# The last norm's factor from a matrix of ones, and two background transfers placed later, in a one-core residual block

## The chip, the core and the metric

The kernel runs on one core of one Trainium2 chip. The engines that appear below are TensorE (PE, with its weight loads PEld), VectorE (DVE), ScalarE (ACT), GpSimd (POOL) and SyncE (SP), which only issues transfers here. Every time is in device microseconds (us) of one execution of the whole program. Before the change the median of three runs is 695.37 us (695.27 to 695.41).

## The reference

One trunk layer on x of 512 tokens by 1024 features, in float32, and a last RMSNorm. What matters here is the second half:

```
h = rms_norm(x, norm_ffn_g)
up = causal_dwconv(h @ w_up, conv_ffn_w)        # 1024 -> 2 * 2816, three taps
a, b = split(up, 2)
x = x + (silu(a) * b) @ w_down                  # 2816 -> 1024
return rms_norm(x, norm_f_g)                    # x / sqrt(mean(x*x) + 1e-6) * g
```

Ahead of it stand a first norm, one wide projection, a short gated convolution, forgetting attention, two sigmoid gates and an output projection w_o.

## The kernel before, in words

**Layout.** Features lie on the 128 partitions, tokens along the free dimension: x is a tile `xm` (also called x1) of 8 blocks of 128 features by 512 tokens. A sum over features is a sum over partitions, so the kernel makes it on TensorE, with a matrix or a column of ones.

**Arithmetic.** Each weight chunk is loaded as float32 (`raw_...`), and split into a high part `wh_...` (ACT, L275) and a rest `wl_...` (DVE, L279). A product is then three matmuls: high by high, rest by high, high by rest. The activations are split in the same way: `gh` and `gl` hold the hidden activations, `x1h` and `x1l` the normed input.

**The stream of weights.** All chunks stand in one list in the order of use. `split()` loads ahead on SP's queue (up to 7 chunks, in buffers of 4 per kind) and makes the two parts of the next chunk. A load waits until its buffer's last chunk has been split. Everything on SP's queue starts in the order in which it stands there.

**Seven products in place of eight.** Many products go through `seven()`, in which a pair of output blocks and input blocks is worked off with seven half-size products on sums of weights and activations. For these a chunk comes in two pieces: `P{n}`, loaded straight from the weights `wst`, and `F{n}` ("full"), which holds sums of weights. Those sums are made in the background in DRAM tiles `f{n}`, two values of n to a tile, by `make_forms()`: a copy into the tile on SP, an adding transfer on POOL, a copy within the tile on SP, an adding transfer on POOL, another copy and another adding transfer. Each of the six waits for the one before it. `slot()` is called at fixed places of the program, counts them, and issues the operations that are due. `GROUPS` gives, for each set of sums, how many n to a tile, the slots of the six operations, and how many slots later the next tile's start.

**The feed-forward part.** The 22 hidden blocks of 128 run in two phases (0 to 11, 12 to 21). Block j is made in `up(j, ...)`, two calls of `slot()` each. A phase ends with steps through `seven()` that multiply by w_down: 12 steps of one P and one F in phase 0 (P18/F18 to P29/F29), with one `slot()` each. The output projection before has 8 slots, so block 11 has slots 30 and 31 and the steps of phase 0 have 32 to 43. Blocks 14 and 16 in phase 1 go through `seven()` too; their sums are the tiles `f30` and `f32` ("phase 1's sums"), which are made during phase 0. The key is `"up1"`.

**Where a phase turns.** Work that takes finished sums out of TensorE's banks waits in a list `later` and is handed out between splits. Entries with the tag `("e",)` belong to blocks that went through `seven()`. At the last block of a phase, `up()` splits the first P chunk; if entries with that tag are still there, it also hands all of them out and splits the first F chunk.

**The end.** The last two output blocks are finished in two halves of 256 tokens. For each half, `ssq3` collects the sums of squares per partition, with the very last block's squares in `sq3_...` apart. `rstd_col()` turns them into a column: matmuls with the squares as weights and one column of ones (L344) put the 256 tokens on partitions, as 128 by 2; ACT takes the root (L350), DVE the reciprocal (L352). `rstd_bc()` (L363) spreads the column back over all partitions with matmuls against the identity into a bank `pb_n31`. `fin_out()` then multiplies the 8 blocks by it in five instructions on DVE (L1412), and sends each piece to DRAM from SP or ACT (L1413). `warm_on(n)` puts n matmuls into TensorE's queue whose results nobody reads.

Of the kernel before, what the change touches and what calls it, by code (L numbers as in the profile page):

```python
# [8 lines left out]
F32 = mybir.dt.float32  # L9
F32R = mybir.dt.float32r  # L10
AF = mybir.ActivationFunctionType
ALU = mybir.AluOpType

P = 128
D = 1024
S = 512
KB = D // P
# [25 lines left out]
PHASES = ((0, 12), (12, NP))  # L43
# [20 lines left out]
DOUBLES = GATES + UPD[0] + STEPS[0] + UPD[1] + STEPS[1]  # L64
NU = [len(GATES), len(GATES + UPD[0] + STEPS[0])]
ND = [NU[i] + len(UPD[i]) for i in range(2)]
GROUPS = {"gate": (2, 4, 1), "up0": (2, 4, 1), "up1": (2, 4, 1), 0: (2, (0, 3, 14, 18, 22, 26), 1), 1: (2, 3, 1)}


@with_exitstack  # L70
def block_kernel(ctx, tc, xT, vecs, wv, win, wmix, wo, wup, wst, wdp, outT):
# [3 lines left out]
    nc = tc.nc  # L75
    PSUM = bass.MemoryType.PSUM

    cp = ctx.enter_context(tc.tile_pool(name="cp", bufs=1))
# [3 lines left out]
    def keep(ins):  # L82
        return tc.keep_in_program_order(ins)

    def bank(i, name):
        return ps.tile([P, S], F32, tag=f"b{i}", name=name)
# [19 lines left out]
    ones = cp.tile([P, P], F32, tag="ones", name="ones")  # L106
# [52 lines left out]
    def after_split():  # L159

        st = ExitStack()
        for ins in order.values():
            st.enter_context(tc.issue_after(ins))
        return st

    def tag_of(k):
        return "raw" if stream[k][0][0] != "F" else "rf" if k >= ff0 else "rg"
# [22 lines left out]
    def make_forms(n0, n1, key, start=0):  # L190

        size, step, shift = GROUPS[key]
        if not start:
            make_forms.slot = 0
        cuts = [n0]
        for n in range(n0 + 1, n1 + 1):
            if n == n1 or n - cuts[-1] == size or len(DOUBLES[n]) != len(DOUBLES[cuts[-1]]):
                cuts.append(n)
        for g, (a, b) in enumerate(zip(cuts, cuts[1:])):
            m = len(DOUBLES[a]) * P  # L200
            f = dr.tile([P, b - a, 4 * m], F32, tag=f"f{a}", name=f"f{a}")
            w = wst[a:b].rearrange("n p c -> p n c")
            x0, x1, x2 = w[:, :, 3 * m : 5 * m], w[:, :, 5 * m : 7 * m], w[:, :, 7 * m : 8 * m]
            for n in range(a, b):
                made[n] = f[:, n - a, :]

            def put(dst, src):
                return lambda: keep(nc.sync.dma_start(dst, src))

            def add(dst, src):  # L210
                return lambda: keep(nc.gpsimd.dma_start(dst, src, accum_op=ALU.add))  # L211

            f0, f1, f2 = f[:, :, : 2 * m], f[:, :, 2 * m : 3 * m], f[:, :, 3 * m :]
            ops = (put(f0, x0), add(f0, x1), put(f1, f[:, :, :m]), add(f1, x1[:, :, m:]), put(f2, f1), add(f2, x2))
            todo_bg.extend((start + (step * k if isinstance(step, int) else step[k]) + shift * g, op) for k, op in enumerate(ops))
        todo_bg.sort(key=lambda w: w[0])
# [7 lines left out]
    def run_later(k, us):  # L224

        n = 0
        while n < len(later):
            if later[n][0] <= k and later[n][1] <= us + 0.1:
                us -= later[n][1]
                with after_split():  # L230
                    later.pop(n)[3]()
            elif later[n][0] <= k:
                return
            else:
                n += 1
# [11 lines left out]
    def flush_only(tags):  # L247

        while n := [n for n, w in enumerate(later) if set(w[2]) & set(tags)]:
            with after_split():  # L250
                later.pop(n[0])[3]()

    def split(hl=None):

        k = len(parts)
        if k == len(stream):
            return
        nm, _, ncol = stream[k]
        load(k + (LOOK if len(raws) > KB else AHEAD))
        if hl is None:  # L260
            hl = []
            for x in "hl":
                if k == 0:
                    wp.tile([P, PADW[x]], F32, tag=f"pad{x}", name=f"pad_{x}")
                w0 = VOFF if k < KB else 0
                hl.append(wp.tile([P, D], F32R, tag=f"w{x}", name=f"w{x}_{nm}", bufs=2)[:, w0 : w0 + ncol])
        hi, lo = hl
        raw = raws[k]
        if k == 0:
            for cs in (slice(VB, S + H), slice(0, VB)):  # L270
                keep(nc.vector.tensor_copy(hi[:, cs], raw[:, cs]))
        elif k == 1:
            keep(nc.vector.tensor_copy(hi, raw))
        else:
            ins = nc.scalar.activation(hi, raw, AF.Copy)  # L275
            order["hi"] = ins.ins
            if k < KB:
                keep(ins)
        ins = nc.vector.tensor_sub(lo, raw, hi.bitcast(F32))  # L279
        order["lo"] = ins.ins  # L280
        if k < KB:
            keep(ins)
        held[tag_of(k)] -= 1
        parts.append((hi, lo))
        if any(("e",) in w[2] for w in later):
            run_later(k, {"u": 4.2, "P": 1.6, "F": 1.2}[nm[0]])
            return
        run_later(k, {"u": 1.7, "P": 1.6, "F": 0.75, "i": 3.0, "m": 3.0, "d": 0 if nm == "dp1" else 2.1}.get(nm[0], 3.5))
# [47 lines left out]
    eps = ex[:, NT : NT + 1]  # L336
# [22 lines left out]
    def rstd_bc(rc, n, bb, name):  # L359

        pb = bank(bb, f"pb_{name}")
        for t in range(n):
            keep(nc.tensor.matmul(  # L363
                pb[:, t * P : (t + 1) * P], rc[:, t : t + 1].to_broadcast([P, P]), ident,
                start=True, stop=True,
            ))
        return pb
# [49 lines left out]
    pb = [pb_[t // 2][:, (t % 2) * 4 * HD : (t % 2 + 1) * 4 * HD] for t in range(NT)]  # L417
# [13 lines left out]
    halves = [slice(0, S // 2), slice(S // 2, S)]  # L431
# [20 lines left out]
    for kb in range(KB):  # L452
        x = xs[kb]
# [320 lines left out]
    for q in (0, 2):  # L774
        f, g = x_sums(slice(q, q + 2))
# [8 lines left out]
    for idx in late:  # L784
        kind, i = divmod(idx, 4)
# [311 lines left out]

    po = None
    make_forms(ND[0], ND[0] + len(STEPS[0]), 0)
    make_forms(NU[1], ND[1], "up1", 20)  # L1100
    for j in range(KB):
        slot()
        if j == 0:
# [32 lines left out]
    ssq3 = xp.tile([P, S], F32, tag="ssq", name="ssq3")  # L1136
# [4 lines left out]
    def up(j, ph, rb2, pu=None):  # L1141
        uu = []

        def tap(i, z):
            u = fp.tile([P, S], F32, tag="fu", name=f"fu{j}{i}", bufs=3)
            taps(u, z, CF + 3 * (2 * j + i))
            uu.append(u)

        if j in SUP[ph]:
            c = 2 * SUP[ph].index(j)  # L1150
            slot()
            seven(
                UPD[ph][c : c + 2], NU[ph] + c, {j: USETS[j]}, lambda q, g: up_form(ph, q, g), of="x",
                done=lambda i, banks, ids: merge(ph, j, banks, ids, rb2, tap, uu),
            )
            slot()
            return
        evacs = []
        for i in range(2):
            slot()  # L1160
            p = pu[i] if pu else block(f"up{2 * j + i}", x1h, x1l, True)
            if i and j + 1 == PHASES[ph][1]:
                split_next()
                if any(("e",) in w[2] for w in later):
                    flush_only((("e",),))
                    split()
            z = [None]

            def mul(i=i, p=p, z=z):
                z[0] = fp.tile([P, S], F32, tag="fz", name=f"fz{j}{i}", bufs=4)  # L1170
                nc.vector.tensor_mul(z[0], p, rb2)

            evac = [(0.7, mul), (1.4, lambda i=i, z=z: tap(i, z[0]))]
            if i:
                evac.append((0, lambda: glu(ph, j, uu)))
            if any(("e",) in w[2] for w in later):
                later.extend((0, us, (("e",), acc.last) if x == 0 else (("e",),), f) for x, (us, f) in enumerate(evac))
            else:
                for _, f in evac:
                    f()  # L1180
# [221 lines left out]
    def fin_col(t, sqs):  # L1402
        s_ = ssq3[:, halves[t]]
        nc.vector.tensor_add(s_, s_, sqs[0])
        return rstd_col([s_, sqs[1]], 2, 3 + t, f"n3{t}", root=True)

    def fin_out(t, rc):
        hs = halves[t]
        pb = rstd_bc(rc, 2, (1, 5)[t], f"n3{t}")[:, : S // 2]
        for g, (a, b) in enumerate(((0, 1), (1, 3), (3, 5), (5, 7), (7, 8))):  # L1410
            y = x1[:, a:b, hs]
            nc.vector.tensor_mul(y, y, pb.unsqueeze(1).to_broadcast([P, b - a, S // 2]))  # L1412
            keep((nc.sync, nc.scalar)[g % 2].dma_start(outT[:, a:b, hs], y))  # L1413
# [10 lines left out]
    plain7(0, 1, kall[:7])  # L1424
    rcA = fin_col(0, sqA)
    plain7(0, 1, kall[7:])
    fin_out(0, rcA)
    sqB = [fin_sum(1, 0)]
    plain7(1, 1, kall[:4])
    for x in range(2):  # L1430
# [1 line left out]
    plain7(1, 1, kall[4:])  # L1432
    sqB.append(fin_sum(1, 1))
    warm_on(3)
    rcB = fin_col(1, sqB)
    warm_on(6)
    fin_out(1, rcB)


_INS = ["xT", "vecs", "wv", "win", "wmix", "wo", "wup", "wst", "wdp"]  # L1440
# [96 lines left out]
```

## Time and profile before

| | |
|---|---|
| median of 3 runs | 695.37 us (695.27 to 695.41) |
| the profiled execution | 694.18 us, of which 692.4 us from the first to the last instruction |
| granted TensorE clock | 0.997 |
| TensorE busy | 683.1 us (99%) |
| VectorE busy | 554.2 us (80%) |
| ScalarE busy | 368.3 us (53%) |
| GpSimd busy | 190.5 us (28%) |

A row of a group view gives the line, the engine, the operation, the tiles as out<-in with their numbers left out, shapes, the count, then busy time and mean ns of one, and the idle time before with what ended it. A row of a timeline gives start, duration, engine, line, tiles and shapes, merged where equal ones follow each other; a matmul in float32 shows as two instructions. Rows with SPq or ACTq are transfers being issued, so their duration is not the transfer's.

### The profile page before, as it was taken

What the parts mean: (1) busy time and instruction counts of PE and PEld (TensorE: products, weight loads), DVE (VectorE), ACT (ScalarE), POOL (GpSimd) and SP (SyncE); (2) the same over time, 40 slices, a digit from 0 to 9 for tenths busy, and PEclk for the clock granted to TensorE, in tenths of its full rate; (3) what the DMA queues carried; (4) which work ended last, traced back from release to release, by engine and by line L of the source; (5) the groups of instructions that cost most, each with busy time, mean ns of one, the idle gap of its engine ahead of it and who ended that gap; (6) DMA issues with size and microseconds to landing.
All of it is one profiled execution on the core that took longest, in us unless ns stands there. A gap on an engine that the chain in (4) does not pass through costs nothing. (4 is left out here: it accounts for less than half of the span.)

```text
span 692.4 us, 14690 instructions
## 1 busy us (share of the span) xinstructions
PE 683.1 (99%) x5936; PEld 680.6 (98%) x5936; DVE 554.2 (80%) x858; ACT 368.3 (53%) x579; POOL 190.5 (28%) x201
## 2 busy tenths in 40 slices
PE   9999999999999999999999999999999999999996
PEld 9999999999999999999999999999999999999995
DVE  6677787877578778769879699998787899988894
ACT  5675755554554444546554555545444544545572
POOL 6134947542020201214400144340100325231000
PEclk9999999999999999999999999999999999999998
DMA  8629999552568586788998498888945996676413
GB/s 308 225 67 293 216 243 204 134 120 92 185 144 221 166 268 205 230 308 213 158 313 241 126 233 222 200 242 231 252 149 167 337 231 157 188 168 182 154 31 122
DMA packets 65012, 137.53 MB, mean 199 GB/s; under 512 B 5760, under 2 KB 30352, under 8 KB 64688
## 3 DMA queue, kind: packets, MB, share of 16 engines
q1 hardware_dynamic: 44664, 107.28, 47.2%
q0 software_dynamic: 18464, 26.03, 23.4%
q10 hardware_dynamic: 1816, 3.29, 1.3%
q8 instruction: 46, 0.75, 0.4%
q14 instruction: 22, 0.18, 0.1%
HBM read 132.31 MB, written 47.71 MB: 260 GB/s over the span
## 5 line engine op out<-in xcount | busy, mean ns | idle before, releaser
L211 POOL DMA_DIRECT2D f<-in_wst_dram x66 | 77.7, 1371 | 27.1 <-DMA f<-f 26.8
L309 PE MATMUL p_up<-x1h,wh_up 128*128 128x256 f32 x416 | 81.2, 276 | 0.0
L309 PE MATMUL p_up<-x1l,wh_up 128*128 128x256 f32 x416 | 81.0, 276 | 0.0
L309 PE MATMUL p_up<-x1h,wl_up 128*128 128x256 f32 x416 | 81.0, 276 | 0.0
L279 DVE TENSOR_TENSOR wl_F<-raw_F,wh_F 128x1024 fp32r<-128x1024 f32 (+1 forms) x42 | 55.9, 1330 | 20.0 <-ACT wh_F L275 20.0
L275 ACT ACTIVATE wh_F<-raw_F 128x1024 fp32r<-128x1024 f32 (+1 forms) x42 | 44.3, 1054 | 39.5 <-PE dn L327 28.7
L309 PEld LDWEIGHTS p_up<-x1h,wh_up 128*128 128x128 f32 x416 | 62.7, 188 | 0.0
L309 PEld LDWEIGHTS p_up<-x1l,wh_up 128*128 128x128 f32 x416 | 62.7, 188 | 0.0
L309 PEld LDWEIGHTS p_up<-x1h,wl_up 128*128 128x128 f32 x416 | 62.6, 188 | 0.0
L309 PE MATMUL p_in<-xgh,wh_in 128*128 128x256 f32 x288 | 56.8, 279 | 0.0
L309 PE MATMUL p_in<-xgh,wl_in 128*128 128x256 f32 x288 | 56.6, 278 | 0.0
L309 PE MATMUL p_in<-xgl,wh_in 128*128 128x256 f32 x288 | 56.5, 278 | 0.0
L279 DVE TENSOR_TENSOR wl_P<-raw_P,wh_P 128x768 fp32r<-128x768 f32 (+1 forms) x42 | 41.7, 992 | 14.7 <-ACT wh_P L275 8.6
L327 PE MATMUL dn<-gh,wh_F 128*128 128x256 f32 x216 | 51.2, 277 | 1.2 <-ACT wh_F L275 1.2
L275 ACT ACTIVATE wh_P<-raw_P 128x768 fp32r<-128x768 f32 (+1 forms) x42 | 35.1, 835 | 32.1 <-PE dn L327 23.2
L327 PE MATMUL dn<-gl,wh_F 128*128 128x256 f32 x216 | 51.0, 276 | 0.0
L1236 POOL TENSOR_TENSOR ge<-fu,fu 128x512 f32<-128x512 f32 x11 | 20.1, 1831 | 110.5 <-DVE fu L570 85.6
L279 DVE TENSOR_TENSOR wl_up<-raw_up,wh_up 128x1024 fp32r<-128x1024 f32 x34 | 43.8, 1288 | 7.4 <-ACT wh_up L275 7.4
L275 ACT ACTIVATE wh_up<-raw_up 128x1024 fp32r<-128x1024 f32 x34 | 35.8, 1054 | 19.4 <-PE p_up L309 9.3
L309 PEld LDWEIGHTS p_in<-xgh,wh_in 128*128 128x128 f32 x288 | 44.7, 188 | 0.7
L309 PEld LDWEIGHTS p_in<-xgl,wh_in 128*128 128x128 f32 x288 | 43.7, 188 | 0.0
L309 PEld LDWEIGHTS p_in<-xgh,wl_in 128*128 128x128 f32 x288 | 43.6, 188 | 0.0
(343 smaller groups left out, 2211.8 us busy)
## 6 DMA issues: line engine op xcount, KB each, us to landing
raw_F<-f SPq DMA_DIRECT2D x41, 512.0 KB, 5.7
raw_up<-in_wup_dram SPq DMA_DIRECT2D x34, 512.0 KB, 5.6
raw_P<-in_wst_dram SPq DMA_DIRECT2D x41, 384.0 KB, 5.4
raw_in<-in_win_dram SPq DMA_DIRECT2D x24, 512.0 KB, 3.6
f<-in_wst_dram POOLq DMA_DIRECT2D x41, 256.0 KB, 6.8
f<-in_wst_dram SPq DMA_DIRECT2D x20, 512.0 KB, 7.1
f<-in_wst_dram POOLq DMA_DIRECT2D x20, 512.0 KB, 9.1
f<-f SPq DMA_DIRECT2D x40, 256.0 KB, 6.5
```

The costliest lines, as they stand in the source:

```text
L211: return lambda: keep(nc.gpsimd.dma_start(dst, src, accum_op=ALU.add))
L275: ins = nc.scalar.activation(hi, raw, AF.Copy)
L279: ins = nc.vector.tensor_sub(lo, raw, hi.bitcast(F32))
L309: keep(nc.tensor.matmul(out[:, cs], w, x[:, cs], start=start and i == 0 and c == 0, stop=stop and i == 2 and c == len(cut) - 1,))
L327: keep(nc.tensor.matmul(out, wl if x == 1 else wh, xl if x == 2 else xh, start=opens and bk not in seen, stop=closes and bk not in left,))
L1236: keep(nc.gpsimd.tensor_mul(ge, a.rearrange(halves_of, h=2), b.rearrange(halves_of, h=2)))
```

## The change

Three edits.

1. **The factor of the last half.** A new `fin_root()` replaces `rstd_col()` and `rstd_bc()` for the second half. Two float32 matmuls with the 128x128 matrix of ones as weights and 256 columns of squares (`ssq3`, then `sq3_11`) put the sum over features into all partitions at once. ACT takes the root over 256 columns from that bank into a tile `rt_n31` in SBUF, DVE takes the reciprocal of 256 columns in place, and the five multiplications read `rt_n31`. The first half is computed as before.
2. **Phase 1's sums.** The operations for `f30` stand at slots 30, 32, 33, 35, 36 and 38 (before: 20, 24, 28, 32, 36, 40), those for `f32` one slot later each.
3. **First full weights.** In `up()`, the first F chunk's `split()` stands ahead of the handing out of the entries with the tag, no longer behind it.

```diff
-GROUPS = {"gate": (2, 4, 1), "up0": (2, 4, 1), "up1": (2, 4, 1), 0: (2, (0, 3, 14, 18, 22, 26), 1), 1: (2, 3, 1)}
+GROUPS = {"gate": (2, 4, 1), "up0": (2, 4, 1), "up1": (2, (0, 2, 3, 5, 6, 8), 1), 0: (2, (0, 3, 14, 18, 22, 26), 1), 1: (2, 3, 1)}
...
-    make_forms(NU[1], ND[1], "up1", 20)
+    make_forms(NU[1], ND[1], "up1", KB + 2 * PHASES[0][1] - 2)
...
             if i and j + 1 == PHASES[ph][1]:
                 split_next()
                 if any(("e",) in w[2] for w in later):
+                    split()
                     flush_only((("e",),))
-                    split()
...
+    def fin_root(sqs):
+
+        pb = bank(4, "pb_n31")[:, : S // 2]
+        s_ = ssq3[:, halves[1]]
+        nc.vector.tensor_add(s_, s_, sqs[0])
+        for i, x in enumerate((s_, sqs[1])):
+            keep(nc.tensor.matmul(pb, ones, x, start=i == 0, stop=i == 1))
+        rt = cp.tile([P, S], F32, tag="rb", name="rt_n31")[:, : S // 2]
+        nc.scalar.activation(rt, pb, AF.Sqrt, scale=1.0 / D, bias=eps)
+        nc.vector.reciprocal(rt, rt)
+        return rt
+
-    def fin_out(t, rc):
+    def fin_out(t, pb):
         hs = halves[t]
-        pb = rstd_bc(rc, 2, (1, 5)[t], f"n3{t}")[:, : S // 2]
...
-    fin_out(0, rcA)
+    fin_out(0, rstd_bc(rcA, 2, 1, "n30")[:, : S // 2])
...
     warm_on(3)
-    rcB = fin_col(1, sqB)
+    rtB = fin_root(sqB)
     warm_on(6)
-    fin_out(1, rcB)
+    fin_out(1, rtB)
```

**At the end, TensorE and VectorE.** TensorE's last rows before the change, from the warming matmuls (`warm_to`) on; `pc_n31` is the column's bank, `pb_n31` the bank that is spread:

```order
L1418 MATMUL warm_to_8773<-gl_3989,gh_3988 128x256 x3
L344 MATMUL pc_n31_8938<-ones_71,ssq3_4528 128x1 x2
L344 MATMUL pc_n31_8938<-ones_71,sq3_11_8931 128x1 x2
L1418 MATMUL warm_to_8773<-gl_3989,gh_3988 128x256 x6
L363 MATMUL pb_n31_8953<-ident_66,rc_n31_8945 128x128 x2
```

The same place of TensorE's queue after the change, from the last product on:

```order
L309 MATMUL pdB7_8767<-gl_3989,wh_dp2_8739 128x256
L1429 MATMUL warm_to_8773<-gl_3989,gh_3988 128x256 x3
L1413 MATMUL pb_n31_8937<-ssq3_4528,ones_71 128x256
L1413 MATMUL pb_n31_8937<-sq3_11_8931,ones_71 128x256
L1429 MATMUL warm_to_8773<-gl_3989,gh_3988 128x256 x6
```

Six small matmuls became two of 256 columns, and nothing on TensorE follows the root any more. VectorE's last rows before, from the last addition to the sums of squares on:

```order
L1404 TENSOR_TENSOR ssq3_4528<-ssq3_4528,sq3_01_8896 128x256
L352 RECIPROCAL rc_n31_8945<-ms_n31_8943 128x2
L1412 TENSOR_TENSOR xm_2605<-xm_2605,pb_n31_8953 128x256
L1412 TENSOR_TENSOR xm_2605<-xm_2605,pb_n31_8953 128x2x256 x3
L1412 TENSOR_TENSOR xm_2605<-xm_2605,pb_n31_8953 128x256
```

and after:

```order
L1411 TENSOR_TENSOR ssq3_4528<-ssq3_4528,sq3_01_8896 128x256
L1416 RECIPROCAL rt_n31_8941<-rt_n31_8941 128x256
L1423 TENSOR_TENSOR xm_2605<-xm_2605,rt_n31_8941 128x256
L1423 TENSOR_TENSOR xm_2605<-xm_2605,rt_n31_8941 128x2x256 x3
L1423 TENSOR_TENSOR xm_2605<-xm_2605,rt_n31_8941 128x256
```

The reciprocal grew from 2 to 256 columns a partition, and the multiplications read SBUF in place of a bank.

**In phase 0's steps, SyncE and GpSimd.** SyncE's queue before, from the load of P22, the fifth step's first chunk, on:

```order
L182 DMA raw_P22_6213<-in_wst_dram 128x768
L182 DMA raw_F22_6243<-f22_3996 128x1024
L182 DMA raw_P23_6268<-in_wst_dram 128x768
L182 DMA raw_F23_6299<-f22_3996 128x1024
L182 DMA raw_P24_6331<-in_wst_dram 128x768
L182 DMA raw_F24_6363<-f24_3997 128x1024
```

and after:

```order
L182 DMA raw_P22_6209<-in_wst_dram 128x768
L182 DMA raw_F22_6239<-f22_3996 128x1024
L208 DMA f30_4000<-f30_4000 256x256
L182 DMA raw_P23_6265<-in_wst_dram 128x768
L182 DMA raw_F23_6296<-f22_3996 128x1024
L208 DMA f32_4001<-f32_4001 256x256
L182 DMA raw_P24_6329<-in_wst_dram 128x768
L182 DMA raw_F24_6361<-f24_3997 128x1024
```

The two first copies within `f30` and `f32` moved here from between the loads of up22 and P18. Further ahead in the same queue, the two copies into the tiles (512 KB each) moved from just ahead of the load of up16 to behind the loads of F18 and F19. The second copies within the tiles stay where they were, ahead of P26 and P27. GpSimd's queue before, in the blocks of phase 0 (`go` and `ge` are its products of the two hidden halves):

```order
L1243 TENSOR_TENSOR go2_5544<-fu50_5469,fu51_5535 128x512
L211 DMA f30_4000<-in_wst_dram 256x1x512
L1236 TENSOR_TENSOR ge3_5616<-fu60_5605,fu61_5611 128x512
L211 DMA f32_4001<-in_wst_dram 256x1x512
L211 DMA f18_3994<-in_wst_dram 256x1x256
```

and after, where the last product of phase 0, `ge5`, stands:

```order
L1236 TENSOR_TENSOR ge5_6040<-fu100_6029,fu101_6035 128x512
L211 DMA f28_3999<-in_wst_dram 256x1x256
L211 DMA f30_4000<-in_wst_dram 256x1x512
L211 DMA f32_4001<-in_wst_dram 256x1x512
L211 DMA f30_4000<-in_wst_dram 256x1x256
L211 DMA f32_4001<-in_wst_dram 256x1x256
```

The two large adding transfers left the stretch between `go2` and `go3` and now stand directly ahead of the two small ones of the same tiles, behind all of GpSimd's products of phase 0.

**The first full weights.** The rows of TensorE, VectorE and ScalarE from the first instruction up to the end's, in names and order, read alike before and after. At both places where edit 3 would act, block 11 and block 21, no entry with the tag is left in the list, so neither of the two exchanged lines runs; the first F chunk is split later, inside `seven()`, in both kernels.

## The prediction

> **What bounds the kernel now.** I read the page's busy times first, then TensorE's waits, then the end of the chain that ended last.
>
> ```profile
> PE 683.1 (99%) x5936; PEld 680.6 (98%) x5936; DVE 554.2 (80%) x858; ACT 368.3 (53%) x579; POOL 190.5 (28%) x201
> PE dn L327 <- ACT wh_F L275: 1.2, 2, 0.7
> PE warm L115 <- DVE ones L107: 1.1, 1, 1.1
> PE dn L327 <- DVE wl_F L279: 0.4, 1, 0.4
> PE p_up L327 <- DVE wl_up L279: 0.2, 1, 0.2
> 683.75 0.78 PE pc_n L344 x8
> 684.54 0.81 PE warm_to L1418 x6
> 685.35 0.47 PE pb_n L363 x4
> 685.82 0.02 issue
> 685.84 0.42 DVE xm L1412
> ```
>
> TensorE is busy for 683.1 of 692.4 us. The next four rows are all of its waits on other engines: 1.2 + 0.4 + 0.2 = 1.8 us apart from the start. So work moved on other engines is worth at most 1.8 us unless it opens a new wait. The last five rows are the end of the chain: from about 683.4 us on TensorE has no products left, and what counts is the string that makes the last factor. The five multiplications start at 685.84, and the output's transfers end the program. Edit 1 acts exactly on this string.
>
> **Edit 1, step by step.** These rows of the timeline are the string. Times are starts and durations.
>
> ```profile
> 683.43 0.38 ACT L1393 ACTIVATE sq<-pdB 128x256 f32<-128x256 f32 x1 [2.72 <-PE pdB L309]
> 683.59 0.50 PE L344 MATMUL pc_n<-ones,ssq 128*128 128x1 f32 x4
> 683.71 0.47 ACT L1394 ACTIVATE xm<-pdB,vec 128x256 f32<-128x256 f32 x1
> 683.95 0.58 PE L344 MATMUL pc_n<-ones,sq 128*128 128x1 f32 x4
> 684.58 0.26 ACT L350 ACTIVATE ms_n<-pc_n,ex 128x2 f32<-128x2 f32 x1 [0.40 <-PE pc_n L344]
> 684.87 0.17 DVE L352 RECIPROCAL rc_n<-ms_n 128x2 f32<-128x2 f32 x1 [2.25 <-ACT ms_n L350]
> 685.19 0.61 PE L363 MATMUL pb_n<-ident,rc_n 128*128 128x128 f32 x4
> 685.84 2.54 DVE L1412 TENSOR_TENSOR xm<-xm,pb_n 128x256 f32<-128x256 f32 x5 [0.80 <-PE pb_n L363]
> ```
>
> Matmuls. A float32 matmul of 256 columns is not in the trace. The four pb_n instructions are its nearest kin: float32, 2 x 128 columns, 0.61 us to the last result, 0.47 us of TensorE by the chain. I price the new one at the same: the first starts at 683.59, when the old first pair did, and holds TensorE until 684.06; the squares are there by then (683.43 + 0.38 = 683.81). The second gives its result 0.61 later, at 684.67. If columns cost nothing beside the weight load, a matmul is two of those four instructions, the second waits for the squares alone as the old one did (683.95), and ends about 0.61 - 2 x 0.11 = 0.39 later, at 684.34. I take the dearer, since twice the columns in an instruction should show; the cheaper is worth 0.33 us and goes into the range.
>
> Root. The old one started 0.05 after its matmuls (683.95 + 0.58 = 684.53 to 684.58). Over 256 columns with one operand a partition, the row at 683.71 took 0.47. So it runs from 684.72 to 685.19, and DVE starts 0.03 later (684.84 to 684.87 before), at 685.22.
>
> Reciprocal, the term that decides. These are the rows for it, from the views of the two lines, in ns (min/median/max), then one of the single-column ones alone with what ended the wait before it, and two plain DVE groups with their mean.
>
> ```profile
> L624 DVE RECIPROCAL m<-m x32: 146/154/164, 57.9 to 167.1; 128x1 f32<-128x1 f32 x32
> L352 DVE RECIPROCAL rc_n<-ms_n x2: 165/166/166, 678.5 to 684.9; 128x2 f32<-128x2 f32 x2
> L624 DVE RECIPROCAL m<-m x1: 164/164/164, 138.4 to 138.4; 128x1 f32<-128x1 f32 x1
>   ACT pp L621: 0.9, 1
> L1290 DVE TENSOR_TENSOR cu<-dn,cz 128x256 f32<-128x256 f32 x7 | 2.9, 413 | 0.0
> L1294 DVE TENSOR_TENSOR xm<-xm,dn 128x512 f32<-128x512 f32 x7 | 4.7, 678 | 0.0
> ```
>
> One column takes 146 to 164, two take 165 or 166. By the extremes a column costs 1 to 20 ns; by the medians (154, 166) 12. But both two-column ones began after a wait (the bracket at 684.87 says 2.25 us idle), and the single-column one that began after a wait, at 138.4, took 164, the top of its range. Like against like a column is then 1 to 2 ns, which is what plain DVE work costs: (678 - 413) / 256 = 1.04 ns. I take 1.04: R = 0.166 + 254 x 0.00104 = 0.43 us. At 2 ns it is 0.67. The dear ends are the rivals below.
>
> Sum. The multiplications would start at 685.22 + R + about 0.03 for the hand-over within DVE, so at 685.25 + 0.43 = 685.68 against 685.84: 0.16 us earlier. They read SBUF in place of a bank; the 128x512 row above is SBUF and bank mixed, and I cost this at nothing. The cheap matmul gives -0.49, R = 0.67 gives +0.08. TensorE's six warming matmuls move ahead of nothing that anybody waits for. DVE has nothing queued behind the reciprocal but the multiplications, and all that follows shifts with them one for one.
>
> [...]
>
> **Edit 2, the moved sums.** Rows: transfer sizes with median us to landing; the extremes for the `f` tiles and for the loads of F in the whole trace; POOL, SP and ACT where the new operations fall; DMA share and GB/s of three stretches (last two numbers).
>
> ```profile
> f<-in_wst_dram POOLq DMA_DIRECT2D x41, 256.0 KB, 6.8
> f<-in_wst_dram POOLq DMA_DIRECT2D x20, 512.0 KB, 9.1
> f<-f SPq DMA_DIRECT2D x40, 256.0 KB, 6.5
> DMA to landing us min/median/max: 3.1/6.9/12.7
> DMA to landing us min/median/max: 3.1/5.7/10.2
> 462.84 3.15 POOL L211 DMA_DIRECT2D f<-in_wst_dram  x3
> 469.86 0.32 SPq L182 DMA_DIRECT2D raw_F<-f  x1
> 471.39 0.33 SPq L182 DMA_DIRECT2D raw_P<-in_wst_dram  x1
> 484.41 0.33 SPq L182 DMA_DIRECT2D raw_P<-in_wst_dram  x1
> 487.31 0.85 ACT L275 ACTIVATE wh_P<-raw_P 128x768 fp32r<-128x768 f32 x1 [1.20 <-PE dn L327]
> 501.58 0.85 ACT L275 ACTIVATE wh_P<-raw_P 128x768 fp32r<-128x768 f32 x1 [1.20 <-PE dn L327]
> 400.00:410.00 10.00, 10.00 (x90) 10.00 (x89) 10.00 (x16) 4.30 (x6) 7.27 (x7) 1.00 0.96 239
> 450.00:460.00 10.00, 10.00 (x91) 10.00 (x90) 8.86 (x12) 4.17 (x6) 2.30 (x2) 1.00 0.83 204
> 480.00:490.00 10.00, 10.00 (x91) 10.00 (x90) 5.80 (x7) 4.55 (x6) 1.03 (x1) 1.00 0.72 218
> ```
>
> Two copies, two large adds and two small copies leave the blocks of phase 0 (DMA share 0.96 at 400 us) for its steps (0.83 and 0.72). In these stretches TensorE is busy 10.00 of 10.00 us, so in the blocks their absence gains nothing. In the steps they add some 2 x 7 + 2 x 9 us of transfers that run beside others, and two waits on SP. The first: the copy behind the load of F22 (469.86) needs the large add, which POOL issues second of three from 462.84, so at about 463.9; with 9.1 it lands at 473. The load of P23 (471.39) leaves 2 us later, and even with 12.7 for the add and 10.2 for itself (the longest of the larger F loads) it is there at 477 + 10 = 487, where ACT splits it at 487.31. The second: the copy ahead of P26 needs the small add behind that first copy: 473 + 6.5 + 6.8 = 487, so P26 leaves at 487 in place of 484.41, with 14 us until its split at 501.58. Behind both stand only loads that are as early. GpSimd's products no longer have the large adds ahead of them; the one that ends phase 0's blocks waits for DVE anyway, so nothing there gets earlier. I cost edit 2 at nothing; the cover is the 14 us or more by which these loads run ahead.
>
> **Edit 3.** No engine's order changes, so its cost is nothing, and the wait that it could have been meant for stays. It is in the waits of the stretch from 460 to 480 us, where phase 0's first F chunk is used:
>
> ```profile
> PE dn L327 <- ACT wh_F L275: 0.7, 1, 0.7
> ```
>
> **Total.** -0.16 + 0 + 0 is about -0.2 us. The profiled execution's 694.18 becomes 694.0. It lies 1.2 us under the median of the runs, 695.37, and the difference is carried over: 695.2.
>
> **The rivals.** For scale: 0.2%, about what a measurement of this kernel can tell from no change, is 1.4 us.
>
> A, forecast: a column costs 1 to 2 ns, edit 2 is hidden. -0.5 to +0.1 us. 0.48.
>
> B, DVE takes two columns at a time: then one and two columns cost the same by nature, the rows above cannot show the price of a pair, and the 12 ns of the medians could be it. R = 0.166 + 127 x 0.012 = 1.7, sum +1.1 us, 696.5. Against it: 1 ns a column needs no such assumption. 0.13, within 0.2%.
>
> C, the other side: a column costs what the medians say. R = 0.166 + 254 x 0.012 = 3.2 us at 12 ns, sum +2.6; at 8 ns R = 2.2 and +1.6. It decides from R = 0.43 + 1.4 + 0.16 = 2.0, that is 7.2 ns a column. For it speaks that a divide is no plain operation, and that the range of the single-column rows allows it; against it the like-for-like pair. 697.0 at 8 ns. 0.27.
>
> [...]
>
> D, SP's queue runs late: if copy and add both need 12.7 us after a first add of 12.7, P26 leaves at 463.9 + 38.1 = 502 and with 5.7 lands 6 us after its split was due. TensorE then waits for most of that: +4 to +6 us, 699 to 701. It decides once the three transfers together need over 501.58 - 5.7 - 463.9 = 32 us, and 1.4 on top; by medians they need 22. 0.07.
>
> E, faster: the weights' waits of 1.2 + 0.4 us go because phase 0's blocks are freed of transfers, with the cheap matmul: -0.49 - 1.2 = -1.7, 693.7. Against it: those waits end on ACT and DVE, not on a transfer. 0.05.
>
> **The numbers.** The time is A's, 695.2. A and B are within 0.2%: 0.61. C and D are slower: 0.34. E is faster: 0.05. The range runs from 694.7 (A with the cheap matmul, and some) to 697.5 (C at 10 ns a column, R = 2.7, sum +2.1); it leaves out E, D and the dearest of C, some 0.15 together. A's own range is 694.8 to 695.5.
>
> **What would show it.** The row of the 256-column reciprocal: 0.4 to 0.7 us for A, 1.7 for B, over 2.0 for C. The two matmuls: the root starting near 684.7 for the dear price, 684.4 for the cheap. The multiplications starting 0.2 us earlier after TensorE's last product. For edit 2: SP's loads of P23 to P27 leave a few us later and TensorE has no new wait between 460 and 530 us; a wait of `dn` on `wh_P` there would be D. For edit 3: the wait of `dn` on `wh_F` between 460 and 480 us stays at 0.7. I am wrong if the reciprocal costs as much a column as a divide in steps, or if the moved transfers slow the loads by more than their 14 us.

## The result and the profile after

The changed kernel takes 696.66 us (median of 20 runs, 695.98 to 697.14), the kernel before 695.12 us (median of 20 runs). The ratio is 1.0020, 95% interval 1.0014 to 1.0027, so 1.0 to 1.9 us slower, and 1.54 us by the medians. I had forecast 695.2, a change too small to be told from none. The profiled execution after is 696.41 us, with a span of 694.6 us.

The page's busy times after, and then all waits of TensorE after (us in total, times, longest):

```profile
PE 682.9 (98%) x5928; PEld 680.5 (98%) x5928; DVE 556.1 (80%) x858; ACT 368.6 (53%) x579; POOL 190.5 (27%) x201
```

```profile
PE dn L327 <- ACT wh_F L275: 1.2, 2, 0.7
PE warm L115 <- DVE ones L107: 1.1, 1, 1.1
PE pa L477 <- DVE wh_v L273: 0.4, 1, 0.4
PE dn L327 <- DVE wl_F L279: 0.4, 1, 0.4
PE p_up L327 <- DVE wl_up L279: 0.2, 1, 0.2
```

VectorE is busy 1.9 us longer. The waits are the old ones, of the old size; new is one of 0.4 us for the first weights (`pa` on `wh_v`), at 8.80 us, far ahead of anything that the change touches. The end of the chain after, from TensorE's last work on:

```profile
684.49 0.88 PE pb_n L1413 x4
685.36 0.02 issue
685.39 0.48 ACT rt_n L1415
685.87 0.02 issue
685.90 1.76 DVE rt_n L1416
687.66 0.02 issue
687.68 0.42 DVE xm L1423
```

VectorE's reciprocal, a row that did not reach the chain before, now is its longest step after TensorE: 1.76 us. The same string in the timeline after:

```profile
684.17 0.38 ACT L1393 ACTIVATE sq<-pdB 128x256 f32<-128x256 f32 x1 [2.69 <-PE pdB L309]
684.33 0.59 PE L1413 MATMUL pb_n<-ssq,ones 128*128 128x256 f32 x2
684.75 0.59 PE L1413 MATMUL pb_n<-sq,ones 128*128 128x256 f32 x2
685.39 0.48 ACT L1415 ACTIVATE rt_n<-pb_n,ex 128x256 f32<-128x256 f32 x1 [0.47 <-PE pb_n L1413]
685.90 1.75 DVE L1416 RECIPROCAL rt_n<-rt_n 128x256 f32<-128x256 f32 x1 [2.52 <-ACT rt_n L1415]
687.68 2.57 DVE L1423 TENSOR_TENSOR xm<-xm,rt_n 128x256 f32<-128x256 f32 x5
```

To compare executions I cut each into five pieces at rows of its timeline: the start (to the first `p_wo` matmul), the body (to the end of the last `pdB` matmul), the string (to the first multiplication), the five multiplications, and the output (to the span's end). In us:

| kernel, one profiled execution each | start | body | string | multiplications | output | span |
|---|---|---|---|---|---|---|
| before | 293.71 | 389.69 | 2.44 | 2.54 | 4.03 | 692.41 |
| after | 294.21 | 389.92 | 3.55 | 2.57 | 4.39 | 694.65 |
| after, again (e8) | 294.29 | 389.78 | 3.55 | 2.57 | 4.40 | 694.60 |
| edit 1 alone (e1) | 294.33 | 389.94 | 3.55 | 2.57 | 4.31 | 694.70 |
| edit 1 alone, again (e9) | 293.66 | 389.92 | 3.55 | 2.57 | 4.35 | 694.06 |
| edit 2 alone (e2) | 293.86 | 390.06 | 2.44 | 2.55 | 4.41 | 693.33 |
| edit 2 alone, again (e10) | 295.29 | 389.94 | 2.44 | 2.55 | 4.62 | 694.84 |
| edit 2, four slots later (e7) | 293.72 | 390.22 | 2.44 | 2.55 | 4.72 | 693.64 |
| first F split ahead (e11) | 293.65 | 389.02 | 2.44 | 2.55 | 4.52 | 692.18 |

The string is the same to 0.01 us in every kernel that has the same one, and it grew by 3.55 - 2.44 = 1.11 us. Start and output scatter by up to 1.6 and 0.7 us between executions, whatever the kernel.

### The profile page after: what moved, and what is told of

Read it like the earlier page. It is cut to its first block, busy times and chain, and to the rows that moved or that the text cites. A ratio compares the mean times of both kernels' runs of the same rounds, so it can differ in the third digit from the quotient of the medians.

```text
span 694.6 us, 14673 instructions
## 1 busy us (share of the span) xinstructions
PE 682.9 (98%) x5928; PEld 680.5 (98%) x5928; DVE 556.1 (80%) x858; ACT 368.6 (53%) x579; POOL 190.5 (27%) x201
```

## The experiments

The theories. **T1**: the width of the reciprocal is the whole loss. **T2**: the moved sums carry a part of it. **T3**: the rest is scatter of the start. Each run had the kernel before beside it on the same chip; its median was 694.9 to 695.0 throughout, unless another number is given.

**Edit 1 alone (e1, again as e9).** Before plus `fin_root()` and its use, without edits 2 and 3.

> The kernel before with edit 1 alone (ones matrix, root and reciprocal over 256 columns). Theory T1, the reciprocal's width is the whole loss: +1.1 us in the string at the end (1.75 us for the reciprocal, the multiplications about 3.55 us after the last product's end in place of 2.44), so the same median as the changed kernel, +1.0 to +1.9 us. Theory T2, the moved sums carry part of the loss: +1.1 us here at most, with the changed kernel 0.4 us slower still. Theory T3, the string gains nor loses and the loss is the start's noise: 0.

> Edit 1 alone, again. T1: +1.1 us, ratio 1.0016, equal to the whole change within its interval. T2: below the whole change by 0.3 us or more.

696.03 us, ratio 1.0013 (1.0004 to 1.0022), and 696.05 us, ratio 1.0016 (1.0007 to 1.0025). In medians that is +1.05 and +1.09 us, close to the string's +1.11.

**Edit 2 alone (e2, again as e10).** Before with the two lines of the slots changed.

> The kernel before with edit 2 alone (the sums for blocks 14 and 16 at slots 30 to 39). T1: no difference, -0.2 to +0.2 us, and no new wait of TensorE between 460 and 530 us. T2: +0.3 to +0.6 us, with a wait of TensorE or a longer stretch between the first step of phase 0 and the last products.

> Edit 2 alone, again. T1: as before the change, ratio 1.0000 within its interval. T2: 0.3 us or more above it, ratio 1.0005 or more, with zero outside the interval.

695.18 us, ratio 1.0003 (0.9995 to 1.0012), and 695.22 us, ratio 1.0008 (0.9999 to 1.0017): +0.20 and +0.26 us in medians. Both intervals hold 1.0000, so neither tells it from no difference.

**The whole change again (e8), on the chip of e9 and e10.**

> The changed kernel once more, beside the next two on the same chip, to weigh its two acting edits against one another. Theory T1 (the reciprocal's width is the whole loss): the string costs +1.1 us over before, so the median stands 1.1 us above that of before (ratio 1.0016), with e9 equal to it and e10 equal to before. Theory T2 (the moved sums carry a part): it stands above e9 by what e10 stands above before, 0.3 us or more, and 1.4 us or more above before.

696.41 us, ratio 1.0024 (1.0015 to 1.0033): 0.36 us above edit 1 alone. That is near what edit 2 alone shows, but the intervals of the two overlap, so this pair by itself leaves T2 open. The body gives no place for such a loss: 389.92 and 389.78 with both edits, 389.94 and 389.92 with edit 1 alone, which cannot act there.

**The reciprocal made cheap (e3).** The changed kernel with a plain instruction of the same shape; the inverse, and so the last norm of the second half, is left out.

```diff
-        nc.vector.reciprocal(rt, rt)
+        nc.vector.tensor_add(rt, rt, rt)
```

> The changed kernel with a plain addition over the 256 columns in place of the reciprocal (the factor is then twice the root and not its inverse, so the last norm is left out for the second half). T1: the addition takes 0.42 us in place of 1.75, so 1.33 us less than the changed kernel, and about 0.2 us less than the kernel before: the time that was predicted. T2: still some 0.2 to 0.4 us above the kernel before, since the moved sums are in it.

695.12 us, ratio 1.0001 (0.9992 to 1.0010). Its timeline:

```profile
686.17 0.43 DVE L1416 TENSOR_TENSOR rt_n<-rt_n 128x256 f32<-128x256 f32 x1 [2.54 <-ACT rt_n L1415]
686.63 2.57 DVE L1423 TENSOR_TENSOR xm<-xm,rt_n 128x256 f32<-128x256 f32 x5
```

The plain instruction takes 0.43 us, just the price at which I had put the reciprocal, and the last `pdB` matmul ends at 684.41, so the string is 686.63 - 684.41 = 2.22 us: 0.22 shorter than before, where I had forecast 0.16. With the one instruction exchanged the loss is gone. (Its median stands 0.14 us above before all the same, 0.36 above what the string gives; the moved sums are in it. More on that below.)

**The price of a reciprocal by width (e4).** Before with reciprocals behind the output: one each of 1 to 512 columns, each fed by a copy on ScalarE, then one that reads a bank, and two back to back.

```diff
+        for n in (1, 2, 3, 4, 6, 8, 12, 16, 32, 64, 128, 256, 512):
+            nc.scalar.activation(ta[:, :n], ta[:, :n], AF.Copy)
+            nc.vector.reciprocal(tb_[:, :n], ta[:, :n])
+            nc.vector.tensor_add(ta[:, :n], ta[:, :n], tb_[:, :n])
```

> The kernel before with extra reciprocals that nobody reads, over 1, 2, 3, 4, 6, 8, 12, 16, 32, 64, 128, 256 and 512 columns in SBUF, and over 128 columns from a bank; they run in and behind the end, so the time of the whole says nothing. T1, six steps of the divide per column: 0.15 us and 6.25 ns a column from a few columns on, 0.35 us at 32, 0.95 at 128, 3.35 at 512, the same from a bank. Rival, two columns at a time with steps of 12 ns: the same slope at even widths, but odd and even neighbours (1 and 2, 3 and 4) equal. Rival, a column costs like a plain operation up to some width: 1 ns a column among the small ones, dearer above.

The groups of VectorE, forms apart (busy us, then mean ns of one; `pw` is a bank):

```profile
L1444 DVE RECIPROCAL wid<-wid 128x512 f32<-128x512 f32 x1 | 3.4, 3353 | 0.7 <-ACT wid L1443 0.7
L1444 DVE RECIPROCAL wid<-wid 128x256 f32<-128x256 f32 x1 | 1.8, 1753 | 0.5 <-ACT wid L1443 0.5
L1448 DVE RECIPROCAL wid<-pw 128x128 f32<-128x128 f32 x1 | 1.0, 958 | 0.1
L1444 DVE RECIPROCAL wid<-wid 128x128 f32<-128x128 f32 x1 | 1.0, 953 | 0.4 <-ACT wid L1443 0.4
L1444 DVE RECIPROCAL wid<-wid 128x4 f32<-128x4 f32 x1 | 0.2, 178 | 0.3 <-ACT wid L1443 0.3
L1444 DVE RECIPROCAL wid<-wid 128x2 f32<-128x2 f32 x1 | 0.2, 165 | 0.0
L1444 DVE RECIPROCAL wid<-wid 128x1 f32<-128x1 f32 x1 | 0.1, 150 | 0.0
```

(3353 - 1753) / 256 and (1753 - 953) / 128 are both 6.25 ns a column, and 153 + 6.25 n gives 3353, 1753, 953 and 178 to the nanosecond; 8, 12, 16, 32 and 64 columns (204, 229, 253, 354 and 552) lie within 1 ns of it. Plain VectorE work costs 1.04 ns a column in this kernel (413 ns for 256 columns and 678 for 512, before), so a column of a reciprocal costs as much as six of plain work. Bank or SBUF makes no difference here (958 and 953 ns, one instruction each). The price that T1 needs is measured by itself; that it comes from six steps is not shown.

One and two columns lie 9 below the line and on it, but both began without a wait, and their rows overlap the ones ahead (the two-column one began at 679.16, where the one ahead ended at 679.24). The kernel before has single columns that began after a wait, as the wide ones here did. Eight of its 32 did, and they took 162 to 164 ns. Two of them, each after 0.5 us of waiting for ScalarE:

```profile
L624 DVE RECIPROCAL m<-m x1: 164/164/164, 99.6 to 99.6; 128x1 f32<-128x1 f32 x1
L624 DVE RECIPROCAL m<-m x1: 164/164/164, 131.9 to 131.9; 128x1 f32<-128x1 f32 x1
```

In all fourteen traces such a column takes 162 to 167 ns, 164 in the median, and not the 159 of the line. So after a wait the second column costs 1 to 2 ns (164, then 165 or 166), and the third and fourth together 12 (178).

**Edit 2, four slots later (e7, traced again as e12 and e13).** Edit 2 with every operation of `f30` and `f32` shifted.

```diff
-    make_forms(NU[1], ND[1], "up1", KB + 2 * PHASES[0][1] - 2)
+    make_forms(NU[1], ND[1], "up1", KB + 2 * PHASES[0][1] + 2)
```

> The kernel before with edit 2 alone, but every operation of f30 and f32 four slots later than the change has them (first copies at slots 34 and 35, second small copies at 42 and 43). It measures the cover of edit 2. Theory V1: the loads of the steps run 14 us or more ahead and SP's queue is late by single microseconds only, so it costs nothing, and the sums are done long before block 14 uses them: ratio 1.000 within 0.001, no wait of TensorE on a P or F part after 500 us that the kernel before lacks. Theory V2: four slots later the waits of the copies for the adds stand ahead of the last loads of the steps and ahead of up1's loads, the cover is gone, and a wait for wh_P, wh_F or wh_up of 1 us or more appears between 500 and 580 us: 696 to 699.

696.19 us, ratio 1.0016 (1.0007 to 1.0026), but its traced execution was the quickest of ten, 695.41 us. Its only row that differs in TensorE's waits is this one (0.2 before):

```profile
PE p_up L327 <- DVE wl_up L279: 0.4, 1, 0.4
```

So no wait for a step's weights came, as V1 says, and still the ratio is beyond V1's 0.001. Two more traces were to show where:

> The kernel e7 (the moved sums four slots later still) once more for its trace: its ten times had a median of 696.2 but the traced execution was the quickest of them, 695.4, and showed no new wait. Theory X1: the extra 1.3 us are waits of TensorE on a part (wl_up, wh_P, wh_F or wl_F) between 460 and 640 us, in an execution of 696 us or more. Theory X2: they are waits at the start (pa on wh_v, before 11 us), the scatter that other kernels show too, and the stretch from the first p_wo to the last pdB takes 389.7 to 390.2 us as before and in the first trace.

> The same kernel as e12 and e7, a third trace. X1: a new wait between 460 and 640 us wherever the time is 696 us or more. X2: the stretch from the first p_wo to the last pdB is the same in all three traces within 0.3 us, and what differs is the start or the output's transfers behind the last multiplication.

695.00 and 695.35 us, where the one run of before beside them took 694.19. Their bodies are 390.10 and 390.14 us, with the first trace's 390.22 longer than any other in the table, and the wait for `wl_up` is 0.4 in all three. That is 0.4 to 0.5 us more body than the trace of before; of this, 0.3 lies at that one wait (0.44 after 0.15 in the timeline), which e11, without edit 2, has as well. As X2 says, the three bodies agree within 0.3. No execution of 696 us or more was traced, so what makes up the rest of the 1.3 us was not seen. That these sums, placed later still, cost something is measured; where is open.

**Edit 3 made to act (e6).** The exchanged lines of edit 3 never run, since no tagged entry is left. Here the F chunk's split is made always.

```diff
                 split_next()
-                if any(("e",) in w[2] for w in later):
-                    flush_only((("e",),))
-                    split()
+                split()
```

> The kernel before with one change: at the last block of each phase the first F chunk is split always, in place of only when entries with the tag are left in the list. This is what the exchanged lines of edit 3 would have done, had they ever run. The question: could it have given anything? Theory U1: the wait of dn on wh_F of 0.7 us near 468.6 and that of 0.5 us near 633.8 exist because ACT makes these parts too late; with the split earlier both go, TensorE's products end 0.7 to 1.4 us earlier, and the time is 694.0 to 694.6 where the kernel before stands at 695.2 (ratio 0.998 to 0.999). Theory U2: ACT and VectorE are the bound there, so the split in front delays gh and gl (which wait behind it on ACT), and the wait is then for gh or gl: the same loss under another name, ratio 1.000 within 0.001, or slower.

698.11 us, ratio 1.0043 (1.0030 to 1.0056): 3.2 us slower, U2 and worse. The two longest of TensorE's waits inside the body, then ScalarE's timeline around phase 0's first F chunk and in the steps of phase 1:

```profile
PE dn L327 <- DVE gl L1261: 1.4, 1, 1.4
PE dn L327 <- ACT wh_F L275: 1.3, 2, 0.7
```

```profile
467.53 0.63 ACT L1229 ACTIVATE fu<-fu 128x512 f32<-128x512 f32 x1 [1.94 <-DVE fu L570]
468.07 1.04 ACT L275 ACTIVATE wh_F<-raw_F 128x1024 fp32r<-128x1024 f32 x1
469.02 0.62 ACT L1260 ACTIVATE gh<-go 128x512 fp32r<-128x512 f32 x1
...
647.09 1.05 ACT L275 ACTIVATE wh_F<-raw_F 128x1024 fp32r<-128x1024 f32 x1
648.03 0.61 ACT L1260 ACTIVATE gh<-go 128x512 fp32r<-128x512 f32 x1
```

The split is written earlier, but ScalarE still does the silu (`fu<-fu`) first, and that waits 1.94 us for VectorE; so `wh_F` is no earlier against TensorE, and its wait stays at 0.7. What did move is the splits of the hidden activations, which are handed out by the count of chunks already split: `gh<-go` fell behind `wh_F`, and TensorE waits 1.4 us, at 650.45, for the `gl` made from it. The body is 392.55 us, 2.9 over before's; that wait, a new one of 0.3 us for `wl_P` and the growth of the old ones come to some 2 us of it, and the rest is in no wait that the view lists.

**The F split in front, and nothing else (e11).** The timeline of before again: ScalarE ahead of that wait, and then, in TensorE's, the first matmul of the steps and the one that waits.

```profile
464.44 1.66 ACT L1262 ACTIVATE gh<-go 128x512 fp32r<-128x512 f32 x3
466.99 0.63 ACT L1231 ACTIVATE fu<-fu 128x512 f32<-128x512 f32 x1 [0.89 <-DVE fu L570]
467.53 1.04 ACT L275 ACTIVATE wh_F<-raw_F 128x1024 fp32r<-128x1024 f32 x1
```

```profile
465.77 0.28 PE L327 MATMUL dn<-gh,wh_P 128*128 128x256 f32 x1
...
468.62 0.38 PE L327 MATMUL dn<-gh,wh_F 128*128 128x256 f32 x1 [0.66 <-ACT wh_F L275]
```

There are two buffers for high parts; the one that `wh_F` needs is free when the last `p_up` matmul gives way to `dn` at 465.77. ScalarE is through with `gh<-go` at 466.10 and then waits 0.89 us for VectorE at the silu, with the split behind it. In e11 the split stands ahead of the silu in phase 0, and ahead of the table load in phase 1; it leaves the handing out of the `gh` parts where it was.

```diff
                 split_next()
...
+                flush_only([("q", x) for x in range(j // 2)])
+                split(early=True)
+                if not ph:
+                    with behind_full(True):
+                        silu = nc.scalar.activation(uu[0], uu[0], AF.Silu)
...
         if j == NP - 1:
-            nc.scalar.activation(tbl, a[: 4 * H, :1], AF.Sqrt, scale=0.0, bias=eps[: 4 * H])
+            with behind_full(True):
+                nc.scalar.activation(tbl, a[: 4 * H, :1], AF.Sqrt, scale=0.0, bias=eps[: 4 * H])
```

`split(early=True)` makes the two parts and hands out nothing from `later`; that is done where F was split before. `behind_full()` has ScalarE issue what stands in it behind `wh_F`.

> The kernel before with the first F chunk of each phase's steps split ahead on ScalarE: in phase 0 directly behind the gh<-go4 parts and ahead of the silu of fu110, in phase 1 ahead of the table load behind the silu of fu210. No other row of ScalarE moves, the gh parts stay ahead of it, VectorE has two rows exchanged and TensorE none. The earlier variant e6 left the silu in front, which waits for VectorE, and pushed gh parts back. Theory W1: the waits of dn on wh_F of 0.7 and 0.5 us are a matter of this order on ScalarE, since the buffer is free when the last p_up matmul ends (465.8 and 631.1 us) and the split of 1.04 us then is done when TensorE wants it: both waits go or shrink to 0.2 us, TensorE's products end 0.8 to 1.4 us earlier, 693.8 to 694.4 where before stands at 695.1, ratio 0.998 to 0.999. Theory W2: the delay lands elsewhere (silu, the taps, wh_P19 or wl_F18 late): the waits return under other names, ratio 1.000 within 0.0005.

693.88 us, ratio 0.9985 (0.9976 to 0.9994): 1.1 us faster than before, and 2.5 us faster than the changed kernel beside it. ScalarE's timeline at the same place, and all of TensorE's waits:

```profile
464.42 1.66 ACT L1287 ACTIVATE gh<-go 128x512 fp32r<-128x512 f32 x3
465.98 1.07 ACT L276 ACTIVATE wh_F<-raw_F 128x1024 fp32r<-128x1024 f32 x1
466.97 0.64 ACT L1178 ACTIVATE fu<-fu 128x512 f32<-128x512 f32 x1
```

```profile
PE warm L115 <- DVE ones L107: 1.1, 1, 1.1
PE p_up L332 <- DVE wl_up L280: 0.4, 1, 0.4
PE dn L332 <- DVE wl_F L280: 0.4, 1, 0.4
PE pa L482 <- ACT xgh L463: 0.3, 1, 0.3
```

`wh_F` starts 1.55 us earlier, the silu starts when it did before, and both waits on `wh_F` are gone. The body is 389.02 us, 0.67 under before's. The two waits had 1.2 us together, and the medians gained 1.1. W1 holds, though TensorE's last product ends only 0.73 us earlier than in the one trace of before (682.67 after 683.40), a little under W1's 0.8.

## Why the prediction was wrong, point by point

**The step that failed** is the reciprocal's term, "R = 0.166 + 254 x 0.00104 = 0.43 us". It measured 1.75 us. That is 1.32 us too little, and it turns the sum of -0.16 into +1.11 with the other terms' small misses. The price of a column came from the step from one column to two, and was carried over 254 more. That step had been read rightly: the row at 138.4 is not the only one that began after a wait, as I wrote, but one of eight, and all eight stand within 2 ns of it. So it was not scatter that misled. The first step is cheap, 1 to 2 ns, and from the third column on each costs 6.25. Its agreement with plain work's 1.04 ns I took for a confirmation, and it was none. The medians, 12 ns, missed to the other side by as much; they mix in the 24 single columns that began without a wait, most of them shorter.

**The rivals.** B's figures (R = 1.7, +1.1 us) are those that came out, and B had named the flaw: "the rows above cannot show the price of a pair". Its mechanism, two columns at a time, stays open. One and two columns at nearly the same price and 12.5 ns for each further pair fit it; a least time of some 164 ns for narrow ones fits as well. The odd widths in e4 (1 and 3) began without a wait, where a single column takes anything from 145 to 166 ns, so they cannot decide. For wide instructions it makes no difference: from 4 to 512 columns e4 shows 6.25 ns a column. C's threshold, 7.2 ns a column, was not reached: e4 measured 6.25. C's 8 ns, and the 10 ns at the end of the range, lie among what the rows allowed (1 to 20 ns), but no run shows either; nor does one show a divide in steps, only what a column costs. The measured 696.66 lies far outside A's own 694.8 to 695.5; the whole range held it only because it was stretched towards C at 10 ns a column, which is not what happened.

B was booked as too small to tell from no change, and that was wrong too: "0.2%, about what a measurement of this kernel can tell from no change" was too coarse. The interval of the result is under half a microsecond to either side, and e1 with its eleven runs already told 1.05 us from nothing.

**The rest of the string** came out as priced. Counted from the last product's end, and set into before's time (0.73 us earlier): the first matmul at 683.60 (forecast 683.59), the second's result at 684.61 (684.67), the root from 684.66 for 0.48 us (684.72 for 0.47), the reciprocal's start at 685.17 (685.22). The dear price for the matmul was the right one. Reading SBUF in place of a bank was worth nothing: 2.57 us for the five multiplications against 2.54.

**Edit 2.** The cover held, with less to spare than I wrote. SyncE's timeline after, from the first copy within `f30` to the load of P26:

```profile
474.67 0.50 SPq L208 DMA_DIRECT2D f<-f  x1
475.26 0.55 SPq L182 DMA_DIRECT2D raw_P<-in_wst_dram  x1
...
478.58 0.50 SPq L208 DMA_DIRECT2D f<-f  x1
479.17 0.56 SPq L182 DMA_DIRECT2D raw_P<-in_wst_dram  x1
...
489.97 0.48 SPq L208 DMA_DIRECT2D f<-f  x1
490.54 0.55 SPq L182 DMA_DIRECT2D raw_P<-in_wst_dram  x1
```

With the execution's own shift of 0.5 us taken off, P23 left 3.4 us later than before, at 475.26 (forecast 2), and P26 5.6 later, at 490.54 (forecast 2.6; the terms as written add up to 486.3, not 487, so 1.9). What I had too small is the small add ahead of P26's copy: GpSimd issued it at 479.92, and it took 10.0 us to land where the sum had 6.8. And I had overlooked that the copy of `f32` ahead of P24 waits too, for the second large add; P24 left 3.8 us later. P26's split is at 502.08, still 11.5 us after its load left; by the time that up24 is loaded (503.95, before 503.45) the queue has caught up, and TensorE has no new wait from 460 to 530 us. D did not come near. Whether edit 2 costs a few tenths without such a wait is taken up below.

**Edit 3** does nothing, as said: the wait of `dn` on `wh_F` is 0.7 us as before. E's condition, that these waits go, was right about the prize (1.2 us; e11 gains 1.1 us by it) and rightly called unrelated to transfers.

**What is left of the loss.** The 0.43 us between the string's +1.11 and the medians' +1.54 were not located. In the profiled executions 0.50 of the difference lies in the start and 0.36 in the output, pieces that scatter as much between executions of other kernels. T3 is likely for those two executions, but the medians should not show it. The medians lean to T2. Less what the string gives, the kernels with edit 2 stand above before by 0.43 (the whole change), 0.34 (e8), 0.36 (e3), 0.20 (e2) and 0.26 us (e10); those without it stand at -0.06 (e1) and -0.02 (e9); and e7, with the sums later still, lost 1.28. Apart from e7 none of them shows it clear of its interval, and no trace shows a place for it. So "I cost edit 2 at nothing" is likely some two to four tenths of a microsecond too small as well, but this is not shown, and how it would come about stays open.

## What to carry to other kernels

Count the columns of an operation that is not plain arithmetic before trading instructions for width: four short steps over 2 columns beat two over 256 here (2.44 us against 3.55 for the string), because a reciprocal's column is 6.25 ns and not 1.04. Where the trace holds only the two narrowest forms of an instruction, the step between them need not be the price of a further column, however cleanly it is measured: here it was 1 to 2 ns, and 6.25 after that. The forecast has to hold the dear end, or a wide one has to be run first. And when an exchange of lines is meant to bring work forward, look at what really runs, and at what stands ahead of it in its engine's queue: the wait of 0.7 us stayed in e6, and went only in e11, where the split was put ahead of the instruction that was itself waiting.

## What was unexpected of the hardware

A float32 reciprocal on VectorE cost 153 ns and 6.25 ns a column in e4, straight to within 1 ns from 4 to 512 columns among those that began after a wait, with 953 ns from SBUF and 958 from a bank for 128. Two columns lie on that line (165 or 166), one column 5 ns above it (164). A second one directly behind another of the same shape took 896 ns in place of 954, so its columns, 128 x 6.25 = 800 ns of it, do not overlap the other's (one instruction).
